# Sums of squares of heads and latents: two products of parts in place of one full float32 product, and scale columns by products of one column

## Chip, core and metric

The kernel runs on one core of a Trainium2 chip. The core has a tensor engine (PE, with its weight loads listed as PEld), a vector engine (DVE), a scalar engine (ACT), GpSimd (POOL), and a sync engine (SP) that issues most of the DMAs. The metric is the device time of one execution in microseconds.

## What is computed

The reference is a decoder trunk of two layers on a residual stream `h` of 512 tokens by 1024 channels, in float32. The change touches the norms inside the four mixers. Cut to that:

```python
def rmsnorm(x, g):
    y = x * lax.rsqrt(jnp.mean(x * x, axis=-1, keepdims=True) + EPS)
    return y * g

for l in range(2):
    h = h + 0.5 * swiglu(rmsnorm(h, ffn1_norm[l]), ...)
    z = rmsnorm(h, mix_norm[l]) @ w_in[l]
    # MLA: latents c_q (256) and c_kv (128), each with a norm of its own
    q = rmsnorm(c_q, q_norm) @ w_uq
    kv = rmsnorm(c_kv, kv_norm) @ w_ukv
    # HGRN2 and retention: four heads of 64 values each, a norm per head
    o = o * lax.rsqrt(jnp.mean(o * o, axis=-1, keepdims=True) + EPS) * norm_g
    o = o - jnp.mean(o, axis=-1, keepdims=True)      # retention only, first
    h = h + concat([mla, spatial_gate, hgrn2, retention]) @ w_out[l]
    h = h + 0.5 * swiglu(rmsnorm(h, ffn2_norm[l]), ...)
    h = h + (p[l] @ w_ple) * sigmoid(rmsnorm(h, ple_norm[l]) @ w_pg)
return rmsnorm(h, final_norm)
```

## The kernel before

The residual stream lies transposed in SBUF: eight tiles `h[k]` of 128 channels by 512 tokens. A norm over channels is therefore a sum over partitions, and the kernel takes it with the tensor engine: a product with a matrix of ones (`onesr`) puts the sum of squares of each token into all 128 partitions. For the heads, `blk` holds two blocks of 64x64 with 1/64 in them, so that each half of the partitions gets the mean over its own head.

**Parts.** Large products are made from parts. `parts` (L137 to L140) copies a float32 tile on ACT into a tile of type float32r (`hi`) and subtracts it on DVE from the source (`lo`). `mm3` (L181 to L186) then issues three products, hi by hi, hi by lo and lo by hi, on L183, L184 and L185. Almost all of the tensor engine's work has this form: the feed-forward products (`gu`, `dx`, `dy`, `dz`, `dn`), the combined input projection (`z`, `n`), the output projection (`y`) and the gates (`pg`, `pp`). Weights come by DMA from SP into `wr`, and ACT (L138) and DVE (L139) split them some chunks ahead.

**Norms of the stream.** `row_rsqrt` (L233) splits the accumulated squares `acc` into the parts `ac` by itself (L236 on ACT, L237 on DVE), multiplies both by `onesr` (L240), and goes on to Ln, Exp and one newton step. It is called eight times in the program.

**Norms inside the mixers.** Two places use a single full float32 product in place of parts:
- `group_norm` (L441): for each half `c` of two heads ACT copies the heads' output from PSUM (L445) and squares it (L446), the tensor engine multiplies the squares by `blk` (L448, tile `gq`), and DVE adds the epsilon term (L449). It runs for HGRN2 and for retention in each layer, so there are eight such products in all. The result `y` is scaled (L457) and later multiplied by the gates (`gated`, L461).
- `latents` (L742): after the chunks for `c_q` and `c_kv` the squares are summed into `acc` (L751 to L755) and `sq` (L760). Two products with `onesr` read as float32 follow (L764, tile `ms`), two in each layer, so four in all. DVE then forms the mean and adds the epsilon term (L765, L766), ACT takes Ln and Exp, and a newton step on DVE (L229 to L231) gives `lr`. The code in this place runs under `urgent`, which raises its priority.

**Scale columns.** Some products have tokens in the partitions, so they need the scale of each token as a column. `columns` (L257) takes four chunks of 128 tokens from the row-wise scale, transposes each on the tensor engine into a 128x128 block of one PSUM bank (L261), and DVE copies the first column of each block (L263). It is called twice in each layer: for the mixer norm (`rc`) and for the latents (`rkvc`).

**Around it.** In the mixers, dense steps (chunks of `z` and `n`) alternate with the levels of the HGRN2 scan: each level has small products of 32x32 (L586, tile `nr`), then DVE work (L598, L630, L631). The order on each engine is made when the program is built: a scheduler takes the instructions by priority and by its own estimate of when their inputs are ready, and gives tiles their buffers. On the chip each engine runs its instructions in that fixed order and waits where an input is late. Temporary tiles of `t2` share six buffers, PSUM tiles of `mps` four.

Of the kernel before, what the change touches and what calls it, by code (L numbers as in the profile page):

```python
# [10 lines left out]
F32 = mybir.dt.float32  # L11
F32R = mybir.dt.float32r
# [4 lines left out]
ALU = mybir.AluOpType  # L17
AX = mybir.AxisListType

P = 128  # L20
D = 1024
T = 512
# [5 lines left out]
NB = T // P  # L28
# [3 lines left out]
HV = 64  # L32
# [28 lines left out]
def trunk(ctx, tc, xT, pT, pos, wgu, wdn, winT, winN, wout, wpg, wpp, wmla,  # L61
          sgw, sgb, vecs, rows, cst, dec, out):
    nc = tc.nc
    pe, act, dve, pool = nc.tensor, nc.scalar, nc.vector, nc.gpsimd

    cp = ctx.enter_context(tc.tile_pool(name="const", bufs=1))
# [10 lines left out]
    def nm(s):  # L77
        uid[0] += 1
        return f"{s}{uid[0]}"

    def unit(dt=F32, shape=(P, 2, T), name="u"):
        return up.tile(list(shape), dt, tag="u", bufs=24, name=nm(name))

    def t2(shape=(P, T), dt=F32, name="t"):
        return tp.tile(list(shape), dt, tag="t", bufs=6, name=nm(name))
# [10 lines left out]
    def mps(name="m"):  # L96
        return pp.tile([P, T], F32, tag="m", bufs=4, name=nm(name))
# [7 lines left out]
    ident = cs[:, K_ID:K_ID + P]  # L105
    caus = cs[:, K_CAUS:K_CAUS + P]
    mk = cp.tile([P, 5, 32], U8, name="mk")
    onesr = cp.tile([P, P], F32R, name="onesr")
    pool.memset(onesr.bitcast(F32), 1.0)
    blk = cp.tile([P, P], F32, name="blk")  # L110
    pool.memset(blk, 0.0)
    for p0 in (0, HV):
        pool.memset(blk[p0:p0 + HV, p0:p0 + HV], 1.0 / HV)
    idb = cp.tile([P, P], BF16, name="idb")
    negb = cp.tile([P, P], BF16, name="negb")

# [7 lines left out]
    def wtile(name):  # L124
        return wp.tile([P, WB], F32R, tag="w", bufs=6, name=nm(name))
# [11 lines left out]
    def parts(hi, lo, src):  # L137
        i = act.copy(hi, src)  # L138
        dve.tensor_tensor(lo, src, hi.bitcast(F32), op=ALU.subtract)  # L139
        return i  # L140
# [47 lines left out]
    def after(i, earlier):  # L188

        tc.add_manual_dep(getattr(i, "ins", i), getattr(earlier, "ins", earlier).name,  # L190
                          mybir.DependencyInfo(mybir.DependencyClass.NoSync, mybir.DependencyReason.SCHED_ONLY),
                          reason="slots in turn")
# [35 lines left out]
    def newton_step(v, r, t):  # L228
        dve.tensor_tensor(t, r, r, op=ALU.mult)  # L229
        dve.scalar_tensor_tensor(t, t, -0.5, v, op0=ALU.mult, op1=ALU.mult)  # L230
        dve.scalar_tensor_tensor(r, t, 1.5, r, op0=ALU.add, op1=ALU.mult)  # L231

    def row_rsqrt(acc, n, last=None, v=None):  # L233

        a = [t2(dt=F32R, name="ac") for _ in range(2)]
        act.copy(a[0], acc)  # L236
        dve.tensor_tensor(a[1], acc, a[0].bitcast(F32), op=ALU.subtract)  # L237
        q = mps("ms")
        for i in range(2):
            pe.matmul(q, lhsT=onesr, rhs=a[i], start=i == 0, stop=i == 1)  # L240
        return ln_rsqrt(q, n, tp.tile([P, T], F32, tag="r", bufs=2, name=nm("r")), last,
                        v is not None and (v, t2(name="rt")))

    def ln_rsqrt(q, n, r, last=None, vt=None):

        v, t = vt or (t2(name="rv"), t2(name="rt"))
        dve.tensor_scalar(v, q, 1.0 / n, EPS, op0=ALU.mult, op1=ALU.add)
        i = act.preload_act_table_set("natural_log_exp_and_others")
        if last is not None:
            after(i, last)  # L250
        after(act.activation(t, v, AF.Ln), i)
        expo[0] = act.activation(r, t, AF.Exp, scale=-0.5)
        after(expo[0], i)
        newton_step(v, r, t)
        return r

    def columns(r, tag):  # L257

        q = mps("rc")
        for i in range(NB):  # L260
            pe.transpose(q[:, i * P:(i + 1) * P], r[:, i * P:(i + 1) * P], ident)  # L261
        c = sp.tile([P, NB], F32, tag=tag, bufs=1, name=nm(tag))
        dve.tensor_copy(c, q[:, 0:T:P])  # L263
        return c

    class Norm:
# [174 lines left out]
    def group_norm(os, vx, gcol):  # L441

        y, v, t = unit(name="y"), unit(name="gv"), unit(name="gt")
        for c in range(2):
            act.copy(y[:, c], os[c])  # L445
            last = act.activation(t[:, c], os[c], AF.Square)  # L446
            q = mps("gq")
            pe.matmul(q, lhsT=blk, rhs=t[:, c], start=True, stop=True)  # L448
            dve.scalar_tensor_tensor(v[:, c], vx, EPS, q, op0=ALU.mult, op1=ALU.add)  # L449
        rr = unit(name="gr")  # L450
        i = act.preload_act_table_set("natural_log_exp_and_others")
        after(i, last)
        after(act.activation(t, v, AF.Ln), i)
        after(act.activation(rr, t, AF.Exp, scale=-0.5), i)
        newton_step(v, rr, t)
        for c in range(2):
            dve.scalar_tensor_tensor(y[:, c], y[:, c], vec[:, gcol + c:gcol + c + 1], rr[:, c], op0=ALU.mult, op1=ALU.mult)  # L457
        return y
# [5 lines left out]
    def mixers(l, norm, done):  # L464
        x = norm.x
        r = norm.scale(True)
        rc = norm.rc

        def tsteps(j):

            w = weights(winT[l, j])
            o = dense("z")
            for k in range(KD):
                i = mm3(o, wpart(w, k * P), xpart(x[k]), k == 0, k == KD - 1)
                if k % 4 == 3:
                    yield i
            return o
# [264 lines left out]
        def latents():  # L742

            cqx = []
            acc = tp.tile([P, T], F32, tag="acc", bufs=1, name=nm("acc"))
            for e in range(2):
                o = yield from tsteps(10 + e)
                with urgent():
                    cqx.append(split(o, vec[:, g0 + e:g0 + e + 1]))
                    if e == 0:  # L750
                        act.activation(acc, o, AF.Square)  # L751
                    else:
                        sq = t2(name="sq")
                        act.activation(sq, o, AF.Square)
                        dve.tensor_tensor(acc, acc, sq, op=ALU.add)  # L755
            o = yield from tsteps(8)
            with urgent():
                ckx = split(o, vec[:, g0 + 2:g0 + 3])
                sq = t2(name="sq")
                act.activation(sq, o, AF.Square)  # L760
                v, t, rr = unit(name="lv"), unit(name="lt"), unit(name="lr")
                for e, (a, n) in enumerate(((acc, 256), (sq, P))):
                    q = mps("ms")
                    pe.matmul(q, lhsT=onesr.bitcast(F32), rhs=a, start=True, stop=True)  # L764
                    dve.tensor_scalar(t[:, e], q, 1.0 / n, None, op0=ALU.mult)  # L765
                    dve.scalar_tensor_tensor(v[:, e], norm.vx, EPS, t[:, e], op0=ALU.mult, op1=ALU.add)  # L766
                act.activation(t, v, AF.Ln)
                act.activation(rr, t, AF.Exp, scale=-0.5)
                newton_step(v, rr, t)
                rkv = rr[:, 1]  # L770
                tabq = t[:, 0]
                dve.scalar_tensor_tensor(tabq, rr[:, 0], MLA_SCALE, tabs["m"], op0=ALU.mult, op1=ALU.mult)
                rkvc = columns(rkv, "rkvc")
            op_ = yield from tsteps(9)
            with urgent():
                tr = t2(name="tr")
                dve.tensor_tensor(tr[64:P], tabs["m"][64:P], r[64:P], op=ALU.mult)
                ta, tb = t2(name="ka"), t2(name="kb")
                dve.tensor_tensor(ta[64:96], op_[64:96], tr[64:96], op=ALU.mult)
                dve.tensor_tensor(tb[64:96], op_[96:128], tr[96:128], op=ALU.mult)  # L780
                krot = t2(name="krot")
                dve.tensor_tensor(krot[64:96], ta[64:96], tb[64:96], op=ALU.add)
                dve.tensor_tensor(krot[96:128], ta[64:96], tb[64:96], op=ALU.add)
            lat.update(cq=cqx, ck=ckx, rkv=rkv, tabq=tabq, rkvc=rkvc, krot=krot)
# [17 lines left out]
        def dense_steps():  # L802
            yield from latents()
            yield from values()
            yield from ret_rot(0, "q")
            yield from ret_rot(1, "k")
# [24 lines left out]
        for b in range(2):  # L831
# [10 lines left out]
            with urgent():  # L842
                for e in range(2):
                    p0 = 64 * e
# [16 lines left out]
        for b in range(2):  # L861
# [27 lines left out]
            for j in range(NB):  # L889
                b0 = (0, 4, 7, 9)[j]  # L890
                for e in range(2):
                    hh = 2 * b + e
                    mla_end = pe.matmul(o[e * HV:(e + 1) * HV, j * P:T], lhsT=va[:, j, hh * HV:(hh + 1) * HV],
                              rhs=pts[e][:, b0:b0 + NB - j], start=j == 0, stop=j == NB - 1)
# [15 lines left out]
        od = [retention(b) for b in range(2)]  # L910

        yd = group_norm(od, norm.vx, C_RET + 2 * l)


# [47 lines left out]
        for m in range(KD):  # L962
            w = weights(wout[l, m])
# [105 lines left out]
    for k in range(KD):  # L1069
        prev = inturn(nc.sync.dma_start(out=h[k], in_=xT[:, k, :]), prev)  # L1070
        norm.x[k] = split(h[k], gain(V_FFN1, k))
        for m in range(2):
            if k % 2 == 0:
                c = slice(k * P, (k + 2) * P)
# [4 lines left out]
    with urgent():  # L1079
        for m in range(2):  # L1080
            w, hi, lo = unit(shape=(P, WB), name="wr"), wtile("wh1"), wtile("wl1")
            for k in range(0, KD, 4):
                c = slice(k * P, (k + 4) * P)
                prev = inturn(nc.sync.dma_start(out=w[:, c], in_=wgu[0, 1, m, :, c]), prev)
                i = parts(hi[:, c], lo[:, c], w[:, c])
# [132 lines left out]
```

## Time and profile before

| | us |
|---|---|
| median of three runs | 2105.12 |
| lowest, highest | 2102.86, 2105.13 |
| the profiled execution | 2102.31 |
| its span, first to last instruction | 2100.5 |

The mean granted clock of the tensor engine was 0.998 of full speed in the profiled execution. Times in a profile are microseconds from the start of the span. "L448" is line 448 of the kernel. A group such as `gq<-gt,blk` names the tile that is written and the tiles that are read, and a number after x counts the instructions. Matmuls are pipelined, so the durations of neighbours overlap, and the step from one start to the next says what a product costs. An idle time is put down to what ended it.

The mixers of the first layer run from about 360 to 622 us, and those of the second from 1396 to 1657 us:

```profile
360.00:622.00 262.00, 260.02 (x2085) 203.31 (x2084) 186.84 (x341) 132.00 (x228) 11.41 (x20) 1.00 0.28 87
1396.00:1657.00 261.00, 259.03 (x2080) 202.46 (x2079) 188.28 (x335) 129.60 (x225) 11.40 (x20) 1.00 0.28 86
```

The columns are start:end and length, the busy time (and number of instructions) of PE, PEld, DVE, ACT and POOL, the granted clock, the DMA share and GB/s.

### The profile page before, as it was taken

The numbers are of one execution on the slowest core, as the hardware profiler recorded it, in microseconds if no ns is written. First come the engines' busy times: TensorE is split into PE (matmuls) and PEld (weight loads), VectorE is DVE, ScalarE is ACT, GpSimd is POOL, SyncE is SP. The second block draws the span as 40 slices with busy tenths as digits, with TensorE's granted clock in tenths as the row PEclk, the third lists the DMA queues.
The fourth block names the chain that finished last, engine by engine and source line by source line (L and its number), as shares of the span: only waits on it lengthen the run. The fifth ranks groups of instructions, "written<-read, shape, count | busy, mean of one in ns | idle before, by whom it ended". The sixth has DMA issues, their size and how long they took to land.

```text
span 2100.5 us, 30812 instructions
## 1 busy us (share of the span) xinstructions
PE 2076.2 (99%) x12380; PEld 1748.5 (83%) x12380; DVE 1391.8 (66%) x2300; ACT 877.5 (42%) x1367; POOL 76.4 (4%) x109
## 2 busy tenths in 40 slices
PE   8999999999999999999999999999999999999997
PEld 6898988877788898988888889888777888889887
DVE  7875845776575765846768567468866658566476
ACT  5433424634644433424544333255344534233252
POOL 0000100001000000100000000000010000000000
PEclk9999999999999999999999999999999999999999
DMA  6452423222142443633225433232222325333231
GB/s 205 133 156 100 121 98 94 100 75 86 56 121 92 131 128 102 149 105 106 100 92 143 117 109 113 91 100 94 68 89 78 109 91 148 113 112 109 87 126 49
DMA packets 79952, 225.71 MB, mean 107 GB/s; under 512 B 9536, under 2 KB 13120, under 8 KB 79808
## 3 DMA queue, kind: packets, MB, share of 16 engines
q1 hardware_dynamic: 66320, 200.98, 29.4%
q0 software_dynamic: 10240, 18.88, 5.8%
q10 hardware_dynamic: 3248, 3.87, 0.6%
q8 instruction: 97, 1.59, 0.3%
q14 instruction: 47, 0.39, 0.1%
HBM read 219.50 MB, written 2.10 MB: 105 GB/s over the span
## 4 chain that ended last, share of the span: by engine, by line
PE 93%; DVE 3%; ACT 1%; issue 1%; DMA 1%; SPq 0%; ACTq 0%; DVEq 0%; POOLq 0%
PE gu L184 15%; PE gu L183 15%; PE gu L185 15%; PE z L183 4%; PE z L184 3%; PE z L185 3%; PE dx L183 3%; PE dx L184 3%; PE dx L185 3%; PE dn L183 2%; PE dn L184 2%; PE dn L185 2%; PE dy L184 1%; PE dy L185 1%; PE dy L183 1%; PE pg L185 1%
## 5 line engine op out<-in xcount | busy, mean ns | idle before, releaser
L138 ACT CAST wh<-wr 128x1024 fp32r<-128x1024 f32 (+3 forms) x307 | 307.8, 1004 | 706.6 <-issue 327.4
L183 PE MATMUL gu<-x,wh 128*128 128x512 f32 x1408 | 547.5, 389 | 5.4 <-DVE g L321 3.0
L184 PE MATMUL gu<-x,wh 128*128 128x512 f32 x1408 | 548.2, 389 | 0.2 <-DVE x L213 0.2
L185 PE MATMUL gu<-x,wl 128*128 128x512 f32 x1408 | 547.8, 389 | 0.0
L139 DVE TENSOR_TENSOR wl<-wr,wh 128x1024 fp32r<-128x1024 f32 (+3 forms) x307 | 356.6, 1163 | 56.3 <-ACT wh L138 52.3
L183 PEld LDWEIGHTS gu<-x,wh 128*128 128x128 f32 x1408 | 264.3, 188 | 60.9 <-DVE g L321 3.4
L184 PEld LDWEIGHTS gu<-x,wh 128*128 128x128 f32 x1408 | 264.3, 188 | 56.0 <-DVE x L213 1.6
L185 PEld LDWEIGHTS gu<-x,wl 128*128 128x128 f32 x1408 | 264.3, 188 | 54.9
L323 DVE TENSOR_TENSOR g<-g,gu 128x512 f32<-128x512 f32 x88 | 60.4, 688 | 247.1 <-PE gu L185 242.3
L184 PE MATMUL dx<-hb,ws 128*128 128x256 f32 x512 | 144.5, 284 | 0.0
L185 PE MATMUL dx<-hb,ws 128*128 128x256 f32 x512 | 144.1, 283 | 0.0
L183 PE MATMUL dx<-hb,ws 128*128 128x256 f32 x512 | 144.1, 285 | 0.0
L138 ACT CAST ws<-wr 128x512 fp32r<-128x512 f32 x128 | 78.4, 619 | 138.6 <-PE dx L185 83.1
L321 DVE TENSOR_TENSOR g<-gu,r 128x512 f32<-128x512 f32 x88 | 60.5, 689 | 103.1 <-PE gu L185 103.0
L183 PE MATMUL z<-x,wh 128*128 128x512 f32 x320 | 127.1, 397 | 0.0
L185 PE MATMUL z<-x,wl 128*128 128x512 f32 x320 | 126.9, 397 | 0.0
L184 PE MATMUL z<-x,wh 128*128 128x512 f32 x320 | 126.4, 395 | 0.0
L138 ACT CAST hb<-g 128x256 fp32r<-128x256 f32 (+1 forms) x128 | 58.8, 459 | 101.9 <-DVE g L337 50.3
L183 PEld LDWEIGHTS dx<-hb,ws 128*128 128x128 f32 x512 | 97.4, 191 | 1.4 <-ACT hb L138 0.2
L184 PEld LDWEIGHTS dx<-hb,ws 128*128 128x128 f32 x512 | 98.0, 191 | 0.4
L185 PEld LDWEIGHTS dx<-hb,ws 128*128 128x128 f32 x512 | 98.0, 192 | 0.0
L139 DVE TENSOR_TENSOR ws<-wr,ws 128x512 fp32r<-128x512 f32 x128 | 87.1, 687 | 10.8 <-ACT ws L138 10.5
(358 smaller groups left out, 3610.0 us busy)
## 6 DMA issues: line engine op xcount, KB each, us to landing
wr<-in_wgu SPq DMA_DIRECT2D x172, 512.0 KB, 3.2
wr<-in_winT SPq DMA_DIRECT2D x40, 512.0 KB, 3.2
s<-in_wdn SPq DMA_DIRECT2D x64, 256.0 KB, 3.8
s<-in_wdn POOLq DMA_DIRECT2D x64, 256.0 KB, 4.3
wr<-in_wdn SPq DMA_DIRECT2D x32, 512.0 KB, 3.6
wr<-in_wdn SPq DMA_DIRECT2D x32, 384.0 KB, 3.1
a<-in_wdn SPq DMA_DIRECT2D x32, 256.0 KB, 5.1
wr<-in_winN SPq DMA_DIRECT2D x16, 512.0 KB, 3.4
```

The costliest lines, as they stand in the source:

```text
L138: i = act.copy(hi, src)
L139: dve.tensor_tensor(lo, src, hi.bitcast(F32), op=ALU.subtract)
L183: i = pe.matmul(o, lhsT=a[0], rhs=b[0], start=start, stop=False, skip_group_check=go_on)
L184: pe.matmul(o, lhsT=a[0], rhs=b[1], start=False, stop=False, skip_group_check=go_on)
L185: pe.matmul(o, lhsT=a[1], rhs=b[0], start=False, stop=stop, skip_group_check=go_on)
L321: dve.tensor_tensor(g, ps[0], r, op=ALU.mult)
L323: dve.tensor_tensor(g, g, ps[1], op=ALU.mult)
```

## The change

A new helper, `summed`, splits its argument with `parts` and multiplies both parts by a given matrix, accumulating into one PSUM tile. `row_rsqrt` calls it in place of its own copy of that code. `group_norm` and `latents` call it in place of their full float32 product, so `blk` becomes a float32r tile (it is filled through a float32 view). In `columns` each transpose of a 128x128 block becomes a full float32 product of the same block with the first column of the identity, which writes one column; DVE then copies four neighbouring columns.

```diff
-    blk = cp.tile([P, P], F32, name="blk")
-    pool.memset(blk, 0.0)
+    blk = cp.tile([P, P], F32R, name="blk")
+    pool.memset(blk.bitcast(F32), 0.0)
     for p0 in (0, HV):
-        pool.memset(blk[p0:p0 + HV, p0:p0 + HV], 1.0 / HV)
+        pool.memset(blk.bitcast(F32)[p0:p0 + HV, p0:p0 + HV], 1.0 / HV)
...
+    def summed(w, acc, name="ms"):
+
+        a = [t2(dt=F32R, name="ac") for _ in range(2)]
+        parts(a[0], a[1], acc)
+        q = mps(name)
+        for i in range(2):
+            pe.matmul(q, lhsT=w, rhs=a[i], start=i == 0, stop=i == 1)
+        return q
+
     def row_rsqrt(acc, n, last=None, v=None):
 
-        a = [t2(dt=F32R, name="ac") for _ in range(2)]
-        act.copy(a[0], acc)
-        dve.tensor_tensor(a[1], acc, a[0].bitcast(F32), op=ALU.subtract)
-        q = mps("ms")
-        for i in range(2):
-            pe.matmul(q, lhsT=onesr, rhs=a[i], start=i == 0, stop=i == 1)
+        q = summed(onesr, acc)
...
         q = mps("rc")
         for i in range(NB):
-            pe.transpose(q[:, i * P:(i + 1) * P], r[:, i * P:(i + 1) * P], ident)
+            pe.matmul(q[:, i:i + 1], lhsT=r[:, i * P:(i + 1) * P], rhs=ident[:, 0:1], start=i == 0, stop=i == NB - 1)
         c = sp.tile([P, NB], F32, tag=tag, bufs=1, name=nm(tag))
-        dve.tensor_copy(c, q[:, 0:T:P])
+        dve.tensor_copy(c, q[:, 0:NB])
         return c
...
             last = act.activation(t[:, c], os[c], AF.Square)
-            q = mps("gq")
-            pe.matmul(q, lhsT=blk, rhs=t[:, c], start=True, stop=True)
+            q = summed(blk, t[:, c], "gq")
             dve.scalar_tensor_tensor(v[:, c], vx, EPS, q, op0=ALU.mult, op1=ALU.add)
...
                 for e, (a, n) in enumerate(((acc, 256), (sq, P))):
-                    q = mps("ms")
-                    pe.matmul(q, lhsT=onesr.bitcast(F32), rhs=a, start=True, stop=True)
+                    q = summed(onesr, a)
                     dve.tensor_scalar(t[:, e], q, 1.0 / n, None, op0=ALU.mult)
```

## The prediction

> **What bounds the kernel now.** I read the page's first part (busy time by engine), then the shares of the chain of work that ended last, and after that the instructions of the three lines that the change touches.
>
> ```profile
> span 2100.5 us, 30812 instructions
> ...
> PE 2076.2 (99%) x12380; PEld 1748.5 (83%) x12380; DVE 1391.8 (66%) x2300; ACT 877.5 (42%) x1367; POOL 76.4 (4%) x109
> ...
> PE 93%; DVE 3%; ACT 1%; issue 1%; DMA 1%; SPq 0%; ACTq 0%; DVEq 0%; POOLq 0%
> ```
>
> The tensor engine is busy in 99% of the span and carries 93% of the chain. So a product that gets shorter where products follow each other closely shortens the run by as much, and work added on DVE (66%) and ACT (42%) costs only where a product waits for it. The next fence is from the view of single lines: instruction, count, shortest/median/longest ns, first and last start.
>
> ```profile
> L448 PE MATMUL gq<-gt,blk x16: 590/592/697, 507.6 to 1611.0; 128*128 128x512 f32 x16
> L764 PE MATMUL ms<-acc,onesr x4: 592/644/697, 433.3 to 1469.0; 128*128 128x512 f32 x4
> L764 PE MATMUL ms<-sq,onesr x4: 590/590/591, 437.0 to 1472.6; 128*128 128x512 f32 x4
> L261 PE MATMUL rc<-cs,r x8: 271/273/332, 379.0 to 1414.6; 128*128 128x128 f32 x8
> L261 PE MATMUL rc<-cs,lr x8: 270/272/329, 448.4 to 1483.9; 128*128 128x128 f32 x8
> ```
>
> The code issues 8 products at L448 (two group norms of two halves in two layers) and 4 at L764; the trace has 16 and 8 records, so a full float32 product is two records. The 16 transposes of L261 (four in each of four calls) are one record each. Durations overlap in a pipelined engine; what a product costs is seen in the starts of its neighbours, in the timeline (start, duration, engine, line).
>
> ```profile
> 510.32 0.39 PE L183 MATMUL uq<-x,wh 128*128 128x512 f32 x1
> ...
> 510.55 1.02 PE L448 MATMUL gq<-gt,blk 128*128 128x512 f32 x2
> ...
> 511.00 0.80 PE L184 MATMUL uq<-x,wh 128*128 128x512 f32 x1
> ...
> 511.64 0.40 PE L185 MATMUL uq<-x,wl 128*128 128x512 f32 x1
> ...
> 511.88 0.40 PE L183 MATMUL uq<-x,wh 128*128 128x512 f32 x1
> ```
>
> A product of parts follows the one before after about 0.23 us (510.32 to 510.55; 511.64 to 511.88 is 0.24). From 510.32 to 511.64 the engine does L183, the two records of L448, and L184: 1.32 - 2 x 0.23 = 0.86 us for the full float32 product.
>
> **Part 1: twelve sums.** Each turns from one product of 0.86 us into two of 0.23: 0.46. That takes 0.40 us off, and 12 x 0.40 = **4.8 us** off the tensor engine. It also adds a copy on ACT and a subtraction on DVE, which the norms of L236 and L237 do already:
>
> ```profile
> L236 ACT CAST ac<-acc x8: 619/620/625, 24.1 to 2033.1; 128x512 fp32r<-128x512 f32 x8
> L237 DVE TENSOR_TENSOR ac<-acc,ac x8: 693/693/694, 24.7 to 2033.8; 128x512 fp32r<-128x512 f32 x8
> ```
>
> So the second product of a sum is ready 0.62 + 0.69 = 1.31 us later than the square. Whoever reads the sum gets it 1.31 - 0.40 = 0.9 us later. For the group norms that is covered, as the retention norm of the first layer shows:
>
> ```profile
> 585.50 1.41 DVE L457 SCALAR_TENSOR_TENSOR y<-y,vec,gr 128x512 f32<-128x512 f32 x2
> ...
> 599.42 2.35 DVE L461 TENSOR_TENSOR y<-y,g 128x1024 f32<-128x1024 f32 x2
> ```
>
> Its result is there at 586.9 and first used at 599.4: 12.5 us of cover for 0.9. If that were gone, 0.9 us per norm would be the cost. The memsets of `blk` change type only and come at the start: nothing.
>
> **Part 2: four calls of `columns`.** Four transposes of 128 columns become four float32 products of one column. First the transposes, in the timeline:
>
> ```profile
> 378.60 0.39 PE L183 MATMUL z<-x,wh 128*128 128x512 f32 x1
> ...
> 379.01 0.66 PE L261 MATMUL rc<-cs,r 128*128 128x128 f32 x4
> ...
> 379.43 0.48 PE L184 MATMUL z<-x,wh 128*128 128x512 f32 x1
> ...
> 379.74 0.40 PE L185 MATMUL z<-x,wl 128*128 128x512 f32 x1
> ```
>
> L184 really runs one step of 0.23 before 379.74, from 379.51; so the four take 379.51 - 379.01 = 0.50 us. A full float32 product of one column is in no row. It will be two records, each with its own load of a 128x128 stationary operand, so eight loads in place of four. The nearest row has the same stationary shape and 64 columns moving; below it, for the low end, one with tiny operands:
>
> ```profile
> 505.36 0.74 PEld L652 LDWEIGHTS kv<-v,kt 128*128 128x128 f32 x6 [0.17 <-issue]
> ...
> 434.35 0.64 PEld L586 LDWEIGHTS nr<-q,k 128*32 128x32 f32 x62 [0.76 <-issue]
> ```
>
> Six loads in 0.74 us are 0.12 each, whatever streams behind them; eight are 0.96, or 0.46 more than the transposes. I take this: 4 x 0.46 = **1.8 us** added. Low end: 0.64 / 62 = 0.01 a load, eight 0.08, so 0.42 less a call and 1.7 us off in all. High end: no overlap at all, each record as long as a lone transpose, 0.27: eight are 2.16, 1.66 more a call, 6.6 us in all. I stand by the middle because its row loads the same 128x128 float32 operand, and the load, not the stream, is what one column doesn't shorten. The copy that follows moves 128x4 before and after: nothing.
>
> [...]
>
> **Part 3: new waits of the tensor engine.** Its instructions run in order, so a sum's product that stands too early holds every product behind it. The norms that already sum parts show the price:
>
> ```profile
> PEld ms L240 <- ACT ac L236: 3.1, 7, 0.5
> ...
> 372.10 0.39 PE L185 MATMUL z<-x,wl 128*128 128x512 f32 x1
> ...
> 372.55 0.50 PE L240 MATMUL ms<-ac,onesr 128*128 128x512 f32 x1
> ...
> 372.89 0.40 PE L183 MATMUL z<-x,wh 128*128 128x512 f32 x1
> ```
>
> In seven of the eight norms the weight load waited for the copy (3.1 us in all; most of it hidden under the product before). On PE, L240 starts at 372.55 where 372.33 was free, and the next product needs 0.34 in place of 0.23: 0.22 + 0.11 = 0.33 us a sum. How close do the products at L448 and L764 stand to their squares now?
>
> ```profile
> 509.68 0.61 ACT L446 ACTIVATE gt<-ov 128x512 f32<-128x512 f32 x1
> ...
> 436.04 0.60 ACT L760 ACTIVATE sq<-z 128x512 f32<-128x512 f32 x1 [1.37 <-DVE x L213]
> ...
> 436.97 1.02 PE L764 MATMUL ms<-sq,onesr 128*128 128x512 f32 x2
> ```
>
> The second sum of a pair is placed 0.26 us (510.29 to 510.55) and 0.33 us (436.64 to 436.97) behind its square; the first has other work before it. So I charge half of the twelve: 6 x 0.33 = **2.0 us**. Ends: 0 (all are placed later, behind other products) and 12 x 0.33 = 4.0. Each sum also takes two of the six buffers that `t2` hands round; a copy that waits for one delays its product in the same way, and lies within these ends.
>
> **Part 4: DVE around the latents.** From the view of stretches (start:end, length, then busy us of PE, PEld, DVE, ACT) and the chain in order of time:
>
> ```profile
> 435.00:440.00 5.00, 5.00 (x30) 3.76 (x21) 4.94 (x9) 0.60 (x1) 0.00 (x0) 1.00 0.32 108
> ...
> 450.00:455.00 5.00, 4.58 (x110) 3.56 (x98) 4.97 (x11) 0.00 (x0) 0.00 (x0) 1.00 0.62 213
> ```
>
> ```profile
> 447.07 1.23 DVE lr L231
> ...
> 452.21 0.70 DVE k L631
> 452.96 0.76 PE nr L586 x50
> ```
>
> Here DVE is full and the chain runs over it: the newton steps of the latents, then the HGRN level, for which the products of L586 wait. The two subtractions (1.39 us) and a chain 0.9 us longer fall just ahead. Two gaps can take them:
>
> ```profile
> 434.12 1.23 DVE L139 TENSOR_TENSOR wl<-wr,wh 128x1024 fp32r<-128x1024 f32 x1 [1.63 <-ACT wh L138]
> ...
> 441.70 0.69 DVE L779 TENSOR_TENSOR ka<-z,tr 32x512 f32<-32x512 f32 x1 [0.92 <-PE z L185]
> ```
>
> 1.63 + 0.92 = 2.55 us of idle time stand against 1.39. But the products before 441.70 also end up to 0.8 us sooner, and then wait for DVE at 452.96 unless it keeps pace. I charge half a subtraction a layer: 2 x 0.35 = **0.7 us**; ends 0 and 2 x 1.31 = 2.6. Behind a late L586 stand all dense products of this stretch. The two ACT copies here meet an engine that is 0.60 us busy in 435 to 440: nothing.
>
> **The sum.** -4.8 + 1.8 + 2.0 + 0.7 = -0.3 us. The profiled execution took 2102.3 us (span 2100.5, and 1.8 around it), 2.8 below the median of the three runs, so it becomes 2102.0, and the median 2105.1 becomes **2104.8 us**. A measurement of this kernel tells about 0.2%, 4.2 us, from no change: the forecast is no change.
>
> **Rivals.** *A: the sums gain and nothing is paid (faster).* Sums are placed late, and a record of one column costs next to nothing: -4.8 + 0 + 0, down to -6.5 with the low end of part 2: 2098.6 to 2100.3 us. For it: no product of L448 or L764 waits for its square now, and L586 shows very short steps. Against it: seven of eight norms wait, and L586 has small stationary operands. [...]
>
> *B: every sum waits and DVE runs late.* 12 x 0.33 + 2.6: -4.8 + 1.8 + 4.0 + 2.6 = +3.6, 2108.7 us. For it: the norms' waits and the full DVE rows; against it: the gaps of 2.55 us.
>
> *C: the one-column products don't overlap (slower).* Place: the four calls of `columns`. Price: load and product one after the other eight times, 6.6 us; with the other terms as forecast -4.8 + 6.6 + 2.0 + 0.7 = +4.5, 2109.6 us. It decides as soon as a call takes over 2.1 us on PE ((4.2 + 4.8 - 2.7) / 4 = 1.6 above today's 0.5). For it: a product this short gives the next load no stream to hide under; against it: L652, whose loads follow every 0.12.
>
> *D: the change doesn't do what it says*, if the parts' products took as long as full float32. L240 is the same operation with the same operand and its neighbours step on after 0.23 to 0.34, so I give it nothing of its own.
>
> **How the numbers follow.** Forecast (own range 2101 to 2109) 0.46, A 0.22, B 0.14, C 0.18. A is faster by over 4.2 us, C slower by over 4.2, the forecast and B lie between: faster 0.22, same 0.46 + 0.14 = 0.60, slower 0.18. The range leaves half of A and half of C out: 2099.5 to 2110.
>
> **What would show it.** Sums: two records a product at L448's new line, and neighbours 0.46 us apart in place of 0.86. Columns: eight records of 128x1 in some 0.96 us. Waits: a row of PE or its loads waiting for `ac`, near 2.0 us over twelve sums. DVE: the wait of L586 for L631 grown by 0.35 a layer. I would be wrong most of all if the order of the mixers' products, which is fixed when the program is built, moved by more than these operations.

## The result and the profile after

| | before, us | after, us |
|---|---|---|
| median of six runs each | 2104.68 | 2117.62 |
| lowest, highest | 2102.86, 2105.13 | 2114.77, 2119.62 |
| the profiled execution | 2102.31 | 2114.77 |
| its span | 2100.5 | 2113.0 |

The ratio is 1.0065, with a 95% interval of 1.0055 to 1.0076: the change makes the kernel 13 us slower. The forecast was 2104.8 us, no change, with a range up to 2110: the time lies above it.

The page of the changed kernel, with the busy times that were read first before:

```profile
span 2113.0 us, 30881 instructions
...
PE 2082.3 (99%) x12396; PEld 1754.2 (83%) x12396; DVE 1397.8 (66%) x2312; ACT 884.0 (42%) x1379; POOL 76.6 (4%) x109
```

PE is busy for 6.1 us more in a span that is 12.5 us longer, and carries 93% of the chain as before. Nothing here names a place: the shares hide it. The instructions of the new lines (view of single lines: count, shortest/median/longest ns, first and last start) are as few and as short as they were meant to be:

```profile
L239 PE MATMUL gq<-ac,blk x16: 392/496/502, 506.5 to 1622.8; 128*128 128x512 f32 x16
...
L265 PE MATMUL rc<-cs,r x16: 250/250/271, 378.4 to 1421.3; 128*128 128x1 f32 x16
```

To find the place I cut the mixers at marks that both chains of waits contain (start, duration, engine, line). The chain of before, then that of after, first layer:

```profile
379.01 0.66 PE rc L261 x4
...
421.66 1.27 PE nr L586 x95
...
473.80 0.63 PE lv L605 x32
...
506.25 0.91 PE ov L665 x13
...
518.92 0.70 PE sc L871 x2
...
571.28 0.86 PE rv L717 x6
...
643.56 0.63 ACT ac L236
```

```profile
378.41 1.05 PE rc L265 x8
...
421.52 1.27 PE nr L589 x95
...
472.72 0.63 PE lv L608 x32
...
505.16 0.91 PE ov L668 x13
...
519.20 0.70 PE sc L873 x2
...
571.51 0.86 PE rv L720 x6
...
649.10 0.63 ACT ac L138
```

| stage, first layer | holds | before, us | after, us | difference |
|---|---|---|---|---|
| `rc` to `nr` | first `columns` | 42.65 | 43.11 | +0.46 |
| `nr` to `lv` | latents, second `columns` | 52.14 | 51.20 | -0.94 |
| `lv` to `ov` | no edit | 32.45 | 32.44 | -0.01 |
| `ov` to `sc` | HGRN norm | 12.67 | 14.04 | +1.37 |
| `sc` to second `rv` | no edit | 52.36 | 52.31 | -0.05 |
| second `rv` to next norm | retention norm, spatial gate, output projection | 72.28 | 77.59 | +5.31 |

The sum is +6.14 a layer. The same marks in the second layer give as much (the last stage +4.98 there), so the two layers hold 12.3 of the 12.5 us. The first `columns` call costs what was forecast, the stage of the latents gained; the loss is at the two group norms, four fifths of it at retention.

What happens there is read in the timelines (start, duration, engine, line, and in brackets the idle time ahead and what ended it). ACT of after, at the second half of the retention norm (`gt` in these lines holds the squares; `wh` and `wl` are the parts of a weight chunk for dense products):

```profile
575.33 0.60 ACT L450 ACTIVATE gt<-ov 128x512 f32<-128x512 f32 x1
575.96 1.28 ACT L454 ACT_TABLE_LOAD   x1
577.25 1.05 ACT L138 CAST wh<-wr 128x1024 fp32r<-128x1024 f32 x1
578.20 0.62 ACT L138 CAST ac<-gt 128x512 fp32r<-128x512 f32 x1
```

The square ends at 575.93, but its copy `ac` starts only at 578.20: the fixed order of ACT has the table load for Ln (1.28 us) and a weight split `wh` (1.05 us) ahead of it. DVE of before, then of after:

```profile
576.41 0.69 DVE L449 SCALAR_TENSOR_TENSOR gv<-vx,gq 128x512 f32<-128x512 f32 x1 [0.63 <-PE gq L448]
...
587.27 1.23 DVE L932 TENSOR_TENSOR vn<-vn,rows 128x1024 f32<-128x1024 f32 x1
```

```profile
578.33 1.23 DVE L139 TENSOR_TENSOR wl<-wr,wh 128x1024 fp32r<-128x1024 f32 x1 [2.37 <-ACT wh L138]
579.47 0.69 DVE L139 TENSOR_TENSOR ac<-gt,ac 128x512 fp32r<-128x512 f32 x1
580.80 0.69 DVE L452 SCALAR_TENSOR_TENSOR gv<-vx,gq 128x512 f32<-128x512 f32 x1 [0.64 <-PE gq L239]
...
591.70 1.21 DVE L934 TENSOR_TENSOR vn<-vn,rows 128x1024 f32<-128x1024 f32 x1
```

`gv` comes 4.39 us later (580.80 against 576.41), and what stands behind it on DVE with it: the norm's newton step, and by 4.43 us the spatial gate's `vn`, which has nothing to do with the norm except that its instructions are interleaved with it on this engine. Of both, 0.23 us were there when the stage began (571.51 against 571.28). PE of before, then of after:

```profile
588.72 1.89 PE L938 MATMUL sg<-vn,ws 128*128 128x256 f32 x8
...
596.41 0.39 PE L183 MATMUL y<-yT,wh 128*128 128x512 f32 x1
```

```profile
593.09 1.89 PE L940 MATMUL sg<-vn,ws 128*128 128x256 f32 x8
...
595.05 0.40 PE L185 MATMUL z<-x,wl 128*128 128x512 f32 x1
...
598.38 0.90 PE L950 MATMUL yT<-cs,yb 128*128 128x128 f32 x4 [2.21 <-DVE yb L944]
600.24 0.47 PE L183 MATMUL y<-yT,wh 128*128 128x512 f32 x1 [0.96 <-ACT yT L209]
...
601.04 0.63 PE L183 MATMUL y<-yT,wh 128*128 128x512 f32 x1
601.47 0.63 PE L184 MATMUL y<-yT,wh 128*128 128x512 f32 x1
...
605.35 0.39 PE L183 MATMUL y<-yT,wh 128*128 128x512 f32 x1
```

The dense `z` products do not depend on `vn`, so PE runs them in the meantime. Before, 22 of them were left to run between `sg` and the first `y`; when `sg` comes at last in the changed kernel, two are left behind it, and then PE stands idle for 2.21 and 0.96 us. After the gap a step takes 0.43 us (601.04 to 601.47) where it took 0.23 before, and from 605.35 on the products last 0.39 us again. The view of stretches shows why (the column ahead of the last two is the granted clock):

```profile
600.00:603.00 3.00, 2.76 (x8) 2.24 (x9) 2.79 (x6) 2.97 (x5) 0.00 (x0) 0.66 0.86 213
603.00:606.00 3.00, 3.00 (x11) 2.38 (x11) 3.00 (x4) 2.75 (x6) 0.00 (x0) 0.77 0.02 3
```

In stretches of 0.1 us the granted clock is 0.50 from 600.9 to 604.4 us and 1.00 before and behind, as the two means say: (0.34 + 0.23) x 3 / 0.5 = 3.4 us of half speed. Twelve products of `y` took 4.31 us instead of 2.76: 1.55 us.

### The profile page after: what moved, and what is told of

It reads as the page before. It is cut to its first block, busy times and chain, and to the rows that moved or that the text cites. A ratio compares the mean times of both kernels' runs of the same rounds, so it can differ in the third digit from the quotient of the medians.

```text
span 2113.0 us, 30881 instructions
## 1 busy us (share of the span) xinstructions
PE 2082.3 (99%) x12396; PEld 1754.2 (83%) x12396; DVE 1397.8 (66%) x2312; ACT 884.0 (42%) x1379; POOL 76.6 (4%) x109
## 4 chain that ended last, share of the span: by engine, by line
PE 93%; DVE 3%; ACT 2%; issue 1%; DMA 1%; SPq 0%; ACTq 0%; DVEq 0%; POOLq 0%
PE gu L184 15%; PE gu L183 15%; PE gu L185 15%; PE z L183 3%; PE z L184 3%; PE z L185 3%; PE dx L183 3%; PE dx L184 3%; PE dx L185 3%; PE dn L184 2%; PE dn L183 2%; PE dn L185 2%; PE y L183 1%; PE n L183 1%; PE dy L185 1%; PE dy L184 1%
```

## The experiments

**Theory 1:** the copy of the sum by parts stands late in ACT's order, and what stands behind the norm on DVE and ACT is late with it; so the loss is at the group norms, and it goes if the copy is put first. Its rivals have the numbers that the expectations use. **Rival 2:** the one-column products cost it. **Rival 3:** the added copies and subtractions cost it themselves, wherever they stand. **Rival 4:** PE waits for the norm's own late result, and not for what is queued behind it. All ratios are to runs of the kernel before on the same chip.

**Parts of the change alone.** First the one-column products by themselves in the kernel before:

```diff
-            pe.transpose(q[:, i * P:(i + 1) * P], r[:, i * P:(i + 1) * P], ident)
+            pe.matmul(q[:, i:i + 1], lhsT=r[:, i * P:(i + 1) * P], rhs=ident[:, 0:1], start=i == 0, stop=i == NB - 1)
...
-        dve.tensor_copy(c, q[:, 0:T:P])
+        dve.tensor_copy(c, q[:, 0:NB])
```

> The kernel before with only the one-column products in `columns`. Theory 1 (the loss comes from the second half of the group norms: its ACT copy stands behind the table load and a weight split, DVE's newton steps and with them the spatial gate come late, and PE runs out of products): the trace of the changed kernel has 43.11 us from the first transposes to the level products where the kernel before has 42.65, so +0.46 a layer there and 0 to 0.46 at the latents: 0.9 to 1.8 us above before, 2105.6 to 2106.5. Rival 2 (the columns cost the 13 us, by their order or their length): 2115 or more. Rival 3 (the added ACT and DVE work itself): same as theory 1 here.

Measured 2104.38 against 2103.39 us, ratio 1.0004 (0.9995 to 1.0013). The stage of the first `columns` grew by 0.46 and 0.51 us (first and second layer), as forecast. The stage with the second call went from 52.14 to 51.84 and from 52.16 to 52.75, with no steady sign. So the columns do not explain 13 us.

Then the sums by parts at the latents alone (transposes and the norms' float32 products as before):

```diff
-                    q = mps("ms")
-                    pe.matmul(q, lhsT=onesr.bitcast(F32), rhs=a, start=True, stop=True)
+                    q = summed(onesr, a)
```

> The kernel before with two products of parts only at the latents; transposes and group norms as before. Theory 1: this part is a gain; from the level products at 421 us to those near 456 the changed kernel needs 33.82 us where before needs 34.78, and 0.46 of that are its columns, so 1.0 to 1.4 us a layer, 2.0 to 2.8 below before: 2102 to 2102.7. Rival 3 (the added copies and subtractions cost more than the products save, wherever they stand): at or above before, 2104.7 or more. Rival 2: same as theory 1 or a little less.

Measured 2102.55 against 2103.39, ratio 0.9997 (0.9988 to 1.0006). The stage fell to 51.56 and 51.67 us from 52.14 and 52.16: 0.5 to 0.6 a layer, half of the 1.0 to 1.4 expected, and less than the 2 x 0.40 that two sums save. A gain of that size is under what the medians tell; the marks show it. What is missing is in the view of waits: there PE's products of the scan (`nr`) wait for the level's `k` on DVE for 0.8 us in the kernel before, twice 0.4, and for 1.6 us in this one, twice 0.8. PE comes sooner to the scan's products and waits 0.4 us a layer longer for the level on DVE.

The same in the retention norm alone, with a flag that leaves the HGRN norm as it was:

```diff
-            q = mps("gq")
-            pe.matmul(q, lhsT=blk, rhs=t[:, c], start=True, stop=True)
+            if two:
+                q = summed(blk, t[:, c], "gq")
+            else:
+                q = mps("gq")
+                pe.matmul(q, lhsT=blk.bitcast(F32), rhs=t[:, c], start=True, stop=True)
...
```

> The kernel before with two products of parts only in the group norm of retention (four sums of the program's twelve). Theory 1: nearly the whole loss is here, 5.3 us a layer between the last retention products and the next norm: 10 to 11 us above before, about 2115, with PE idle before the yT transposes and the granted clock below 1 behind it. Rival 2: within 1 us of before. Rival 3: a third of the loss, 4 us above before.

Measured 2115.45 against 2103.39, ratio 1.0056 (1.0043 to 1.0070). Four products carry 12.1 us. Its last stage took 78.65 us, 1.1 more than in the whole change; the granted clock was 0.50 in both stretches of 3 us from 600 to 606 (0.66 and 0.77 above), with 0.90 and 0.96 in the stretches ahead of them and behind, so it was at half speed for 6.8 us, twice as long.

And in the HGRN norm alone, by the same flag:

> The kernel before with two products of parts only in the group norm of HGRN2 (four of the twelve sums), the table load where the change has it. Theory 1: the HGRN stage (from the last 13 products of ov to the first scores) takes 14.0 us in place of 12.7, as in the changed kernel, nothing else moves: 2.7 us above before, ratio 1.0008 to 1.0018. Rival 3 (the added work as such): the same as the retention norm cost, 10 us.

Measured 2104.95 against 2102.65, ratio 1.0010 (1.0001 to 1.0019); the stage of that norm took 14.04 and 14.17 us against 12.67. The last stage stayed at 72.26.

**The late copy.** The changed kernel with one edit: the table load of the group norm follows the copy of the second half in place of its square.

```diff
...
-        parts(a[0], a[1], acc)
+        copied[0] = parts(a[0], a[1], acc)
...
             q = summed(blk, t[:, c], "gq")
+            last = copied[0]
...
         i = act.preload_act_table_set("natural_log_exp_and_others")
         after(i, last)
```

> The changed kernel with one edge moved: the table load of each group norm is ordered behind the ACT copy of the second half in place of behind its square. All sums, columns and added work stay. Theory 1: the second copy runs right after its square, the group norms lose nothing, and the sums show their gain: 10 to 13 us below the changed kernel, 2102 to 2106. Rival 3 (the added work itself): stays above 2112. Rival 2 (columns): stays above 2112.

Measured 2102.28 against 2103.39, ratio 0.9996 (0.9987 to 1.0005). The loss is gone. ACT in its timeline:

```profile
575.38 0.62 ACT L139 CAST ac<-gt 128x512 fp32r<-128x512 f32 x1
576.08 1.05 ACT L139 CAST wh<-wr 128x1024 fp32r<-128x1024 f32 x1
577.14 1.28 ACT L456 ACT_TABLE_LOAD   x1
```

The same three instructions in another order: the copy starts 0.03 us after its square (575.35) in place of 2.27. But the build moved more than these. On DVE all four scalings of `vn` now stand directly behind `gv`, ahead of the norm's newton steps:

```profile
578.89 1.38 DVE L934 TENSOR_SCALAR vn<-uv,s,s 128x256 f32<-128x256 f32 x4
581.26 1.23 DVE L230 TENSOR_TENSOR gt<-gr 128x1024 f32<-128x1024 f32 x1 [0.99 <-ACT gr L459]
```

So at the retention norm this run changes two things at once, the place of the copy and that of `vn`. The last stage is 71.93 us (72.28 before), the granted clock 1.00 in each stretch of 3 us from 588 to 612, and the HGRN stage 12.76; there DVE's order is that of the changed kernel, so the 1.3 us come with the earlier copy. No product, copy or subtraction was taken away, so the products and the copies' own time are not what cost 13 us: rivals 2 and 3 are out.

**What waits behind the norm.** The changed kernel, with the gate's `vn` raised in priority and the copy left late:

```diff
+            with urgent():
                 dve.tensor_scalar(vn[:, i], UV(i)[:, 256:512], ...
...
+        with urgent():
             dve.tensor_tensor(vn, vn, rw.unsqueeze(1).to_broadcast([P, NB, 256]), op=ALU.mult)
```

> The changed kernel with the four scalings and the gain of the spatial gate (tile vn) at a higher priority, which puts them on DVE behind the second gv and ahead of the newton steps of the retention norm. The second ACT copy stays behind the table load, so the norm itself comes as late as in the changed kernel. Theory 1 (the late norm costs only because vn stands behind it on DVE): sg starts at about 586 to 588 in place of 593, PE doesn't run out of products, the 5.3 us a layer of this stage go, and the 1.4 us a layer at the HGRN norm stay: 2106 to 2108. Rival 4 (the late norm itself, through the gated products at the end of the stage, is what PE waits for): stays above 2114.

Measured 2106.65 against 2102.51, ratio 1.0019 (1.0009 to 1.0028). DVE:

```profile
582.05 0.69 DVE L452 SCALAR_TENSOR_TENSOR gv<-vx,gq 128x512 f32<-128x512 f32 x1 [0.64 <-PE gq L239]
582.65 1.38 DVE L933 TENSOR_SCALAR vn<-uv,s,s 128x256 f32<-128x256 f32 x4
...
586.10 1.22 DVE L936 TENSOR_TENSOR vn<-vn,rows 128x1024 f32<-128x1024 f32 x1
```

This layer's norm stands 1.25 us later in this run, table load, copy and `gv` alike, so `gv` is as late behind its square as in the changed kernel. Yet the last stage is 73.26 us: 4.3 of its 5.3 us are back once `vn` stands ahead of the newton step (4.05 us behind `gv` in place of 10.90). The norm's own result being late costs little, 1.0 us of this stage, so rival 4 is out. What is queued behind it costs. The run with the table load moved, where the scalings of `vn` stand ahead of the newton steps too but the copy is in time, has 71.93 us: with the copy go 1.3 us more. A run with the copy in time and `vn` left behind the newton steps was not made.

**The clock.** The changed kernel, with nine products between the two groups of `yT` transposes whose result nobody reads:

```diff
...
+            if c == 0:
+                f = mps("fill")
+                for n in range(9):
+                    fill = pe.matmul(f, lhsT=onesr, rhs=x[0][:, 0], start=True, stop=True)
...
```

> The changed kernel with nine products of 128x512 whose result nobody reads, placed on PE between the two groups of yT transposes, where the changed kernel leaves PE idle for 2.2 us. Nothing else in the order of that place is moved. Theory 1 counts 1.55 us a layer of the loss as the lower granted clock behind the gap (12 products of y in 4.31 us where 12 x 0.23 = 2.76 would do): with the gap filled the clock stays at 1 and the run is 3 us shorter, about 2114.5, though PE does more. If the clock has another reason than the idle time, the time stays at 2117 to 2118.

Measured 2114.52 against 2102.51, ratio 1.0050 (1.0035 to 1.0066). PE and one stretch:

```profile
600.92 0.81 PE L950 MATMUL yT<-cs,yb 128*128 128x128 f32 x4 [0.21 <-DVE yb L944]
602.69 0.47 PE L183 MATMUL y<-yT,wh 128*128 128x512 f32 x1 [0.96 <-ACT yT L209]
```

```profile
601.00:604.00 3.00, 2.04 (x10) 1.55 (x11) 3.00 (x7) 1.91 (x3) 0.54 (x1) 1.00 1.01 222
```

The transposes are no earlier relative to `sg` (its first `sg` starts at 595.54, 2.45 later than in the changed kernel, and its first `y` too, 602.69 against 600.24), but the clock stays at 1.00 (third number from the end). The last stage is 75.96 us in both layers, 1.63 and 1.30 less than in the changed kernel. So of the 5.3 us about 1.5 are the clock after the gap, and the rest is the gap and what leads to it.

**The columns within the change.** The changed kernel with the transposes put back:

> The changed kernel with the transposes back in columns; the order of all engines stays the same but for the copies around it. Theory 1: 0.46 us a layer at the mixer norm and up to that at the latents, so 0.9 to 1.8 below the changed kernel, 2115.8 to 2116.7. Rival 2: back at 2105.

Measured 2117.43 against 2102.51, ratio 1.0065 (1.0052 to 1.0079): the same as with the one-column products, where 0.9 to 1.8 us less had been expected. The first `columns` stage is back at 42.62 us, but the latents' stage is 51.64, longer than the 51.20 of the changed kernel: there PE waits 0.8 us a layer for the scan's level on DVE, as with the latents' sums alone. In the changed kernel that wait of PE isn't in the view of waits: the 0.46 us of one-column products stand in its place. Four calls of `columns` come to about nothing in this kernel: in the first layer 0.49 lost at the first call (43.11 against 42.62) and 0.44 regained at the second.

**Versions meant to be faster.** Transposes, sums by parts everywhere, and the table load behind the copy:

> All twelve sums by parts, the table load of a group norm behind the copy of its second half, and the transposes kept. Theory 1: what the table load's new place gave, plus the columns' 0.9 to 1.8: 1.5 to 3.5 us below before on the same chip, ratio 0.9983 to 0.9993. If the sums' gain is lost in waits whatever the order, the ratio is 1.000 or above.

Measured 2101.89 against 2102.51, ratio 0.9996 (0.9987 to 1.0005). That is 0.6 us below before, less than the 1.5 to 3.5 expected: of 4.8 us that twelve sums save on PE only a part is seen. At the HGRN norm none is: the stage is 12.75 us against 12.67. The trace of before shows what sets that stage, on ACT:

```profile
512.33 1.06 ACT L453 ACTIVATE gt<-gv 128x1024 f32<-128x1024 f32 x1 [0.74 <-DVE gv L449]
...
514.49 1.05 ACT L847 COPY kh<-krot 64x1024 f32<-64x1024 f32 x1
```

The copies `kh`, on which the attention's first `sc` hangs, stand behind the norm's Ln and Exp, and these behind `gv`. Here too work is held by the norm only because it shares its engine. So the last pair moves the rest of the group norms (table load, Ln, Exp, newton step, scaling): for HGRN behind the second `kh` copy, for retention behind `vn`.

```diff
...
-        yc = group_norm(oc, norm.vx, C_HG + 2 * l)
+        gc = group_norm(oc, norm.vx, C_HG + 2 * l)
...
         with urgent():
-            act.copy(kt[64:P], krot[64:P].unsqueeze(1).to_broadcast([64, 2, T]))
+            kh_end = act.copy(kt[64:P], krot[64:P].unsqueeze(1).to_broadcast([64, 2, T]))
+        yc = group_rest(*gc, kh_end)
...
-        yd = group_norm(od, norm.vx, C_RET + 2 * l)
+        gd = group_norm(od, norm.vx, C_RET + 2 * l)
...
+        yd = group_rest(*gd, gelu_end)
         yb = unit(shape=(P, NB, 256), name="yb")
```

With sums by parts in all twelve places, and transposes in `columns`:

> All twelve sums by parts, transposes kept, and what follows the sum in the two group norms (table load, Ln, Exp, newton step, scaling) moved: for HGRN2 behind the two kh copies, for retention behind the spatial gate's vn. Theory 1, part two (in the HGRN stage the scores wait for kh, and on ACT Ln and Exp of the late norm stand ahead of kh, so that the sums' 0.8 us a layer can't show there): that stage gets 1 to 2 us a layer shorter than before, and with the 0.8 us a layer that the sums gave with the table load moved the run is 3 to 6 us below before, ratio 0.997 to 0.9985. If PE's products bound that stage, it stays at 12.7 us and the ratio is 0.999 to 1.000.

Measured 2096.18 against 2102.65, ratio 0.9965 (0.9951 to 0.9978): faster than both kernels. ACT:

```profile
509.27 0.62 ACT L138 CAST ac<-gt 128x512 fp32r<-128x512 f32 x1
509.92 1.04 ACT L853 COPY kh<-krot 64x1024 f32<-64x1024 f32 x1
...
515.00 1.28 ACT L458 ACT_TABLE_LOAD   x1
```

The HGRN stage takes 9.82 us in place of 12.67, the latents' 51.43 in place of 52.14, the last one 72.22; 0.33 is lost from `sc` to `rv`. That is -2.85 - 0.71 - 0.06 + 0.33 = -3.3 a layer, 6.6 in all, against 6.5 measured. The HGRN stage gained more than the 1 to 2 us expected.

The same move with the float32 products of before, to see what the sums are worth in it:

> The kernel before (full float32 products, transposes) with the same move of the rest of both group norms. Theory 1, part two: it gets the gain of the order alone, 2 to 4 us below before, ratio 0.998 to 0.999, and stands 1 to 2 us above the kernel with the same order and sums by parts. If the order gives nothing without the parts, it is at before.

Measured 2100.17 against 2102.65, ratio 0.9986 (0.9977 to 0.9995). The move alone gives 2.5 us; 2100.17 - 2096.18 = 4.0 us more come from the sums by parts, where Part 1 had 4.8 and the expectation of this run 1 to 2. The HGRN stage takes 10.96 us here, so the move gives 1.71 us of its 2.85 and the sums 1.14, which were hidden as long as ACT set that stage. At retention the move gives nothing: the last stage is 72.53 us, 0.25 longer than before.

## Why the prediction was wrong, step by step

- **Part 1, the step that failed.** The forecast said that whoever reads a sum "gets it 0.9 us later", that 12.5 us cover this at the retention norm, and so put nothing into the sum for the group norms. The stages that hold them grew by 13.0 us in two layers. Both halves failed. The copy and subtraction were taken at their durations, 1.31 us, as if they started when the square ends; the copy started 2.27 us late behind a table load and a weight split, the subtraction stood behind that weight's other half, and `gv` came 4.39 us later. At the HGRN norm the run that moved the table load shows the copy's place as the cause. At retention that run moved `vn` too, so the copy's part there is read from the timelines and not shown by an edit of its own. And the 12.5 us were counted to the reader of the norm's result (L461). The instructions queued behind the norm's steps on DVE, `vn` above all, have no such cover: raising `vn` gave back 4.3 us with `gv` still late. At the HGRN norm, for which the forecast shows no cover, there was none: `kh` stands right behind the norm's Exp on ACT (514.49).
- **Part 1, its arithmetic** stands: 0.40 us a sum on PE. It is seen at the latents (0.5 to 0.6 us a layer beside a wait longer by 0.4, for two sums), and as 4.0 of 4.8 us where the order doesn't throw it away. At HGRN the stage was set by ACT's Ln, Exp and `kh`, so that with the copy in time the gain was hidden, and with the copy late the stage was 1.37 us longer.
- **Part 2, columns: +1.8 forecast, about 0 in all.** A call cost 0.46 to 0.53 us where PE sets the pace (first `columns`), the 0.46 of the sum; at the latents it took the place of PE's wait for the scan's level, which the forecast had put down in Part 4 without seeing that the two would cover each other. Rival C (no overlap, 6.6 us) is out: at the second call of the changed kernel the eight records start at 449.15 and the next product at 450.13, 0.98 us.
- **Part 3, waits: +2.0 forecast.** The timeline of PE in the changed kernel, at the second half of the HGRN norm:

```profile
510.56 0.50 PE L239 MATMUL gq<-ac,blk 128*128 128x512 f32 x1 [0.20 <-ACT ac L138]
511.29 0.49 PE L239 MATMUL gq<-ac,blk 128*128 128x512 f32 x1 [0.22 <-DVE ac L139]
513.16 0.50 PE L183 MATMUL uq<-x,wh 128*128 128x512 f32 x1 [1.38 <-DVE qh L841]
```

  PE waits 0.20 and 0.22 us for the parts, near the price set, and then 1.38 us for `qh`, which is queued behind the norm on DVE (0.22 us in the kernel before). The view of waits has PE itself waiting for `ac` at two of the twelve sums only, one in each layer, 0.8 us in all. Looking for waits for `ac` was looking at the small ones.
- **Part 4, DVE at the latents: +0.7 forecast, right for the sums alone, nothing in the whole change.** With the latents' sums alone the wait for the level grew by 0.4 us a layer, where the forecast had 0.35. In the whole change the wait is gone, since the one-column products fill it.
- **Rival A** (nothing is paid) is out by the sign, and **rival D** (parts as slow as full float32) by the step: the `gq` product at 507.92 in the changed kernel is followed by the next at 508.15, 0.23 us.
- **Rival B** (every sum waits, DVE late at the latents) had the right sign and the wrong place. The last sentence of the forecast, that it would be wrong most of all if the order fixed at build time moved by more than the operations themselves, is near to what happened, yet the range gave it no room.

The extra time is thus, of 12.3 us found by the marks in both layers: 10.3 in the last stage, 2.7 at the HGRN norm, 1.0 at the first columns, -1.9 at the latents, 0.2 elsewhere. Not settled: why the build puts `vn` behind the newton step in one kernel and ahead of it in another. The retention norm's sums alone met half speed for longer than the whole change did, which need not come from the kernel: the last section shows that the same order meets it differently in its two layers.

## What to carry to other kernels

When an edit puts a small instruction on a busy in-order engine, ask where in that engine's order it will stand and what is fixed ahead of it (here a table load and a weight split), not only how long it takes. When you look for cover, follow not just the reader of the late result but every instruction queued behind the late one on its engine, up to the tensor engine's next product that hangs on one of them. And count what filler PE has left: the loss began when the dense products that run in the meantime were used up.

## What the runs showed of the hardware

In the changed kernel the gap of PE cost more than its length. The last dense product before the gap starts at 595.05 and the next at 600.24; between them stand only eight transposes and idle times of 2.21 and 0.96 us, and the granted clock then fell to 0.50 for 3.4 us, 1.55 us of loss. With nine unread products in the same gap the clock stayed at 1.00 in every stretch of 3 us from 588 to 612 of the first layer, and the last stage took 75.96 us in both layers.

The order of the instructions alone does not decide it. In the changed kernel the gap has the idle times 2.21 and 0.96 us in both layers, and the clock is at 0.50 for 3.4 us in both; but in the first layer from 600.9 to 604.4, where it begins 0.7 us behind the first `y` (600.24), and in the second from 1642.0 to 1645.4, 0.6 us ahead of it (1642.61). At the HGRN norm its idle times are 0.20, 0.22 and 1.38 us in both layers, and the clock stays at 1.00 (508 to 520 and 1546 to 1561). In the run with the sums in the HGRN norm alone, PE has the same idle times at that norm in both layers: 0.20, 0.23 and 1.38 us in the first, 0.19, 0.23 and 1.38 us in the second. The first layer keeps full clock; in the second the granted clock is 0.50 from 1554 to 1557 us, 3.4 us at half speed in all. The stretches at half clock that were read at the norms are 3.4 us long, or 6.8 with the sums in the retention norm alone.

What sets off such a stretch was not shown. No run here put dense products in place of the eight transposes alone, so their part is not told from that of the idle times; the gap at the HGRN norm has no transposes in it.
